# The sample's 64x64 triangular inverses built from 16-blocks instead of 32-blocks

## The chip, the core and the metric

The kernel runs on one core of one Trainium2 chip. The metric is the device time of one execution in microseconds. The engines it uses are TensorE (PE: matrix products, with weight loads as PEld), VectorE (DVE), ScalarE (ACT), GpSimd (POOL) and the queues that issue transfers (SP). Each engine runs its own list of instructions in order and waits on semaphores for the others.

## What is computed

Two layers of a mixed trunk run on 640 tokens: 128 context tokens and 512 sample tokens. In each layer a projection feeds a short convolution, a windowed attention and a gated delta rule ("DeltaNet") in both directions; then come an output projection and a SwiGLU block. The part that the change touches is the delta rule's chunk solve. With chunks of 64 tokens:

```
lmat = einsum('bhnid,bhnjd->bhnij', kb, kc) * dec_strict        # strictly lower triangular
eye  = jnp.eye(CHUNK)
rhs  = concatenate([vc * bc, kb * exp(gc)], axis=-1)
sol  = triangular_solve(lmat + eye, rhs, lower=True, unit_diagonal=True)
```

The kernel forms the inverse of `lmat + eye` itself, for every chunk, head and direction. The sample has 8 chunks, 4 heads and 2 directions, thus 64 inverses of 64x64 in each layer; the context has 2 chunks, thus 16.

## The kernel before

Tokens lie in 5 tiles of 128: tile 0 is the context (group 0, `nt=1`), tiles 1 to 4 the sample (group 1, `nt=4`). A string of letters per layer (`SEQ`) names the stages in the order in which they are written: `Y` and `y` the decays, `A` and `B` the gram matrices of the keys of sample and context, `n` a DeltaNet projection, `l`/`L` the normalisation of keys, `I` and `J` the two halves of the sample's inverses, `i` all of the context's, `E` scalars, `c` tables, `q` queries, `g` and `h` the q-gram of sample and context, `d` steps of the transposed projection for the attention and gates, `s` and `z` steps of the recurrent scan. A list scheduler in the framework then sets the order in which the instructions of all stages stand on each engine, so that a stage's rows lie among those of its neighbours. Around the change the string reads `...DYAInynlndnEcBqdJghqsddds...disf...`.

The weights come in as f32 and are split on chip in a high part (`whi`, a cast on ACT, L172) and a low part (`wlo`, a subtraction on DVE, L173). Every product of 128x128 blocks is thus three matmuls: L199, L201 and L202 for the form with 320 columns, L616, L617 and L618 for the form with 256. These fill TensorE for nearly all of the time. Everything else that TensorE does in this stage is small: transposes against `ident` (L661, L813), grams of 64x64 tiles (L841), and the 32x32 tiles of the inverses.

The sample's inverses before (`invert32_a`, `invert32_b`): the two 32x32 diagonal blocks of each 64x64 matrix lie one per partition, after a copy into `Ld` (L987) and a transpose into `Ls` (L989, L990). A forward substitution then builds `Ts` in 31 steps of two DVE instructions each (L999 multiplies, L1001 subtracts), every step on what the step before wrote. `invert32_b` transposes `Ts` back into `DD` (L1008, L1009) and `TTq` (L1010, L1011), copies `DD` into `adx` (L1018), multiplies by the off-diagonal blocks on TensorE (L1025, 64 matmuls of 32x32 into the buffer `pkq`), brings the product back (`X`), copies the diagonal blocks into place (`MK`, L1036), multiplies again (L1047, 64 matmuls) and writes the last blocks (L1053).

The context's inverses (`invert_a`, `invert_b` with `gi=0`) already go by 16-blocks: a substitution of 15 steps (L887, L889) on both 16-blocks of a 32-block at once, transposes (L898 to L901), then on TensorE a product with `Ld` (L913), DVE's `Xs` (L916), two more products (L927 into `pmx`, L934 into `pkq`), ACT's `adx` (L937), copies of the finished 32-blocks from `pkq` into `MK` (L943, on DVE and ACT by turns), and from there the step from 32 to 64 as above (L952, L955, L967, L973). So each operation of the changed code runs in the kernel before too, for a group of a quarter of the width.

Buffers in PSUM: `pkq` has one, `pmx` two and `pmm` two. The q-gram (`gram`) also uses `pkq`: four matmul groups, L841, each followed by DVE's L846, which must have read `pkq` before the next L841 can write it.

Of the kernel before, what the change touches and what calls it, by code (L numbers as in the profile page):

```python
# [12 lines left out]
AF = mybir.ActivationFunctionType  # L13
ALU = mybir.AluOpType
# [94 lines left out]
def hybrid_trunk_kernel(  # L109
# [8 lines left out]
    V, A, G, PE = nc.vector, nc.scalar, nc.gpsimd, nc.tensor  # L118
    mm = PE.matmul
# [28 lines left out]
    def pkq():  # L148
        return ps.tile([128, 2, 512], F32, tag="kq", name="pkq", bufs=1)
# [429 lines left out]
    def mixer(l, mp, hs, early_half, fill, first, later):  # L579
# [4 lines left out]
        def wk(dt=F32, name="wk", shape=(128, 1024)):  # L584
            return mp.tile(list(shape), dt, tag="wk", name=name, bufs=WK_BUFS)
# [4 lines left out]
        def sm(tag, name, n, bufs):  # L590
            return mp.tile([128, n], F32, tag=tag, name=name, bufs=bufs)
# [36 lines left out]
        kk_, vv, kqT, MK, MQ = [], [], [], [], []  # L628
# [263 lines left out]
        def invert_b(gi, nt, LT):  # L892
            Ld, Ts = LT
            nu = 4 * nt
            TT = MK[gi]
            TTq = square(flat("TTq"))
            DD = sm("s2", "DD", 512, 2).rearrange("p (u j) -> p u j", j=16)
            V.transpose(DD[0:64].rearrange("p u j -> p j u"), Ts[0:64, :, 0:16].rearrange("p x y -> p y x"))  # L898
            V.transpose(DD[64:128].rearrange("p u j -> p j u"), Ts[64:128, 16:32])
            V.transpose(TTq[0:64].rearrange("p u i -> p i u"), Ts[0:64])  # L900
# [71 lines left out]
                    dst = TT[w_:w_ + 32, :, :, d, (1 - d) * 32:(2 - d) * 32].rearrange("p t h i -> p (t h) i")  # L972
                    A.activation(dst, po[w_:w_ + 32, 0:nu * 32].rearrange("p (u i) -> p u i", i=32), AF.Copy, scale=-1.0)  # L973

        def invert32_a(gi, nt):
            eng = V
            nu = 4 * nt
            Ld = wk(name="Ld", shape=(128, 32, 32))
            if gi == 0:
                G.memset(Ld, 0.0)  # L980
            for d in range(2):
                for I in range(2):
                    for c2 in range(2):
                        src = MK[gi][c2 * 64 + I * 32:c2 * 64 + I * 32 + 32, :, :, d, I * 32:(I + 1) * 32]
                        dst = Ld[d * 64 + I * 32:d * 64 + I * 32 + 32, :, c2 * nu:(c2 + 1) * nu]
                        cpe = A.copy if (d + I + c2) % 2 else V.tensor_copy
                        cpe(dst.rearrange("p i u -> p u i"), src.rearrange("p t h i -> p (t h) i"))  # L987
            Ls = wk(name="Ls", shape=(128, 32, 32))
            V.transpose(Ls[0:64].rearrange("p x y -> p (x y)"), Ld[0:64].rearrange("p i u -> p (i u)"))  # L989
            V.transpose(Ls[64:128].rearrange("p x y -> p y x"), Ld[64:128])  # L990
            Ts = wk(name="Ts", shape=(128, 32, 32))
            tsf = Ts.rearrange("p x y -> p (x y)")
            G.memset(tsf, 0.0)
            G.memset(tsf[:, 0:1024:33], 1.0)
            for y in range(31):
                n = 31 - y
                tmp = sm("e1", "tmp", 256, 2)
                tv = tmp[:, 0:n * (y + 1)].rearrange("p (x c) -> p x c", c=y + 1)
                eng.tensor_tensor(out=tv, in0=Ls[:, y + 1:32, y:y + 1].to_broadcast([128, n, y + 1]),  # L999
                                  in1=Ts[:, y:y + 1, 0:y + 1].to_broadcast([128, n, y + 1]), op=ALU.mult)  # L1000
                eng.tensor_tensor(out=Ts[:, y + 1:32, 0:y + 1], in0=Ts[:, y + 1:32, 0:y + 1], in1=tv, op=ALU.subtract)  # L1001
            return Ts

        def invert32_b(gi, nt, Ts):
            nu = 4 * nt
            TTq = wk(name="TTq", shape=(128, 32, 32))
            DD = wk(name="DD", shape=(128, 32, 32))
            V.transpose(DD[0:64].rearrange("p u j -> p j u"), Ts[0:64].rearrange("p x y -> p y x"))  # L1008
            V.transpose(DD[64:128].rearrange("p u j -> p j u"), Ts[64:128])  # L1009
            V.transpose(TTq[0:64].rearrange("p u i -> p i u"), Ts[0:64])  # L1010
            V.transpose(TTq[64:128].rearrange("p u i -> p i u"), Ts[64:128].rearrange("p x y -> p y x"))  # L1011

            adx = sm("s2", "adx", 512, 2)[:, 0:nu * 32].rearrange("p (u j) -> p u j", j=32)
            for d in range(2):
                for c2 in range(2):
                    r = c2 * 64 + d * 32
                    q_ = d * 64 + d * 32
                    (A.copy if c2 else V.tensor_copy)(adx[r:r + 32], DD[q_:q_ + 32, c2 * nu:(c2 + 1) * nu])  # L1018
            px = pkq()[:, 0]
            for u in range(nu):  # L1020
                t, hq = divmod(u, 4)
                for c2, d in ((0, 1), (0, 0), (1, 1), (1, 0)):
                    r = c2 * 64 + d * 32
                    w_ = c2 * 64 + (1 - d) * 32
                    mm(px[w_:w_ + 32, u * 32:(u + 1) * 32], lhsT=MK[gi][r:r + 32, t, hq, d, (1 - d) * 32:(2 - d) * 32],  # L1025
                       rhs=adx[r:r + 32, u], start=True, stop=True)
            X = sm("s2", "X", 512, 2)
            A.copy(X[:, 0:nu * 32], px[:, 0:nu * 32])
            X = X[:, 0:nu * 32].rearrange("p (u j) -> p u j", j=32)
            TT = MK[gi]  # L1030
            for d in range(2):
                for I in range(2):
                    for c2 in range(2):
                        dst = TT[c2 * 64 + I * 32:c2 * 64 + I * 32 + 32, :, :, d, I * 32:(I + 1) * 32].rearrange("p t h i -> p (t h) i")
                        src = TTq[d * 64 + I * 32:d * 64 + I * 32 + 32, c2 * nu:(c2 + 1) * nu]
                        (A.copy if (d + I + c2) % 2 else V.tensor_copy)(dst, src)  # L1036
            for d in range(2):
                for c2 in range(2):
                    z0 = c2 * 64 + (1 - d) * 32
                    G.memset(TT[z0:z0 + 32, :, :, d, d * 32:(d + 1) * 32], 0.0)  # L1040
            po = pkq()[:, 0]
            for u in range(nu):
                t, hq = divmod(u, 4)
                for c2, d in ((0, 0), (0, 1), (1, 0), (1, 1)):
                    r = c2 * 64 + (1 - d) * 32
                    w_ = c2 * 64 + d * 32
                    mm(po[w_:w_ + 32, u * 32:(u + 1) * 32], lhsT=X[r:r + 32, u],  # L1047
                       rhs=TT[r:r + 32, t, hq, d, (1 - d) * 32:(2 - d) * 32], start=True, stop=True)
            for d in range(2):
                for c2 in range(2):  # L1050
                    w_ = c2 * 64 + d * 32
                    dst = TT[w_:w_ + 32, :, :, d, (1 - d) * 32:(2 - d) * 32].rearrange("p t h i -> p (t h) i")
                    A.activation(dst, po[w_:w_ + 32, 0:nu * 32].rearrange("p (u i) -> p u i", i=32), AF.Copy, scale=-1.0)  # L1053


        KTs = mp.tile([128, 2, 2, 640], F32R, name="KTs", bufs=1)
        KTp = mp.tile([128, 2, 2, 128], F32R, name="KTp", bufs=1)
# [142 lines left out]
        early, oos, held = [], [], []  # L1200
# [282 lines left out]
        for op in SEQ[l]:  # L1483
            if op in 'AB':
                gram(1 if op == 'A' else 0, 1)
            elif op in 'Ll':
                l2(1 if op == 'L' else 0, 1)
            elif op in 'Yy':
                decays(1 if op == 'Y' else 0)
            elif op in '23':  # L1490
                dn_post(int(op), ps_[int(op) - 2])
            elif op == 't':
                z_tile(next(tg))
            elif op == 'D':
                decay_scalars()
            elif op == 'c':
                tables()
            elif op == 'E':
                scan_scalars()
            elif op == 'I':  # L1500
                held.append(invert32_a(1, 4))
            elif op == 'J':
                invert32_b(1, 4, held.pop())
            elif op == 'i':
                invert_b(0, 1, invert_a(0, 1))
            elif op == 'n':
                dn_proj(next(ng))
            elif op in 'gh':
                gi = 1 if op == 'g' else 0
                l2(gi, 0)  # L1510
                gram(gi, 0)
            elif op == 'q':
                queries(next(qg))
            elif op == 'k':
                keys()
            elif op == 'm':
                make_mix()
            elif op == 'f':
                fill(FN)
            elif op == 'w':  # L1520
                part_out(next(wg))
            elif op in 'op':
                dn_output(1 if op == 'o' else 0)
            else:
                drain({'s': s1g, 'z': s0g, 'a': ag, 'd': dg}[op], 1)
# [59 lines left out]
    for l in range(depth):  # L1585
# [6 lines left out]
        with tc.tile_pool(name=f"f{l + 1}", bufs=1, reuse_waits="tile") as fp:  # L1592
# [182 lines left out]
            held = pkq()  # L1775
# [102 lines left out]
```

## Time and profile before

| what | value |
|---|---|
| device time, three runs | 1776.96, 1778.72, 1785.07 us; median 1778.72 |
| profiled execution | 1782.25 us, span 1780.5 us |
| mean granted TensorE clock | 0.974 |
| TensorE busy | 94% of the span |
| weight loads | 84% |
| VectorE busy | 70% |
| ScalarE, GpSimd busy | 44%, 9% |

The shares are means over stages. The stage with the sample's inverses lies from about 98 to 205 us in layer 0 and from about 970 to 1075 us in layer 1. PEclk in a view of windows is the clock that TensorE was granted there, as a share of its full 2.4 GHz; 0.50 is the lower level of 1.2 GHz.

### The profile page before, as it was taken

Reading aid. Unit: us, or ns where it says so; the run is one execution under the profiler, and the core shown is the slowest. Engines: PE = TensorE matmul, PEld = TensorE weight load, DVE = VectorE, ACT = ScalarE, POOL = GpSimd, SP = SyncE. Lnnn points to the kernel's source line nnn. Section 1 sums busy time; section 2 is a strip of 40 time slices with the busy share of each in tenths; the row PEclk is TensorE's granted clock in tenths of the full one; section 3 lists DMA queues with packets and bytes.
Section 4 is the critical chain, followed back from the end, with each engine's and each line's share of the span. In section 5 each row is a group of like instructions: output and inputs, shape, how many; then the busy total and the mean of one; then the engine's idle time right before and its main releaser. Section 6 shows DMA issues by size and latency. Waiting matters only on the chain. (4 is left out here: it accounts for less than half of the span.)

```text
span 1780.5 us, 34163 instructions
## 1 busy us (share of the span) xinstructions
PE 1676.7 (94%) x13677; PEld 1497.3 (84%) x13677; DVE 1242.5 (70%) x2764; ACT 782.7 (44%) x1620; POOL 156.3 (9%) x270
## 2 busy tenths in 40 slices
PE   5998999999999999999999989999998999999998
PEld 3887875478899999999988879655888999999998
DVE  3699767665966767666677994886578766667654
ACT  3555244544643433434355442555365343434332
POOL 1111012102300000000032001120041000000000
PEclk8999999999999999999999989999999999999999
DMA  8512224555534223222232222445722222222212
GB/s 280 187 37 78 72 87 129 185 178 164 155 119 131 81 74 96 72 83 73 71 99 75 63 58 67 151 143 164 233 63 84 83 73 82 83 84 84 73 59 60
DMA packets 207693, 188.42 MB, mean 106 GB/s; under 512 B 12782, under 2 KB 182702, under 8 KB 207534
## 3 DMA queue, kind: packets, MB, share of 16 engines
q1 hardware_dynamic: 190656, 170.71, 31.2%
q10 hardware_dynamic: 16878, 15.53, 2.8%
q8 instruction: 108, 1.77, 0.4%
q14 instruction: 51, 0.42, 0.1%
HBM read 168.64 MB, written 17.56 MB: 105 GB/s over the span
## 5 line engine op out<-in xcount | busy, mean ns | idle before, releaser
L172 ACT CAST whi<-raw 128x1024 fp32r<-128x1024 f32 (+1 forms) x102 | 100.0, 981 | 166.5 <-PE pmx L201 73.5
L173 DVE TENSOR_TENSOR wlo<-raw,whi 128x1024 fp32r<-128x1024 f32 (+1 forms) x102 | 115.9, 1138 | 26.5 <-ACT whi L172 26.0
L202 PE MATMUL pmm<-hh,wlo 128*128 128x320 f32 x336 | 109.4, 327 | 6.6 <-DVE wlo L173 6.5
L199 PE MATMUL pmm<-hh,whi 128*128 128x320 f32 x336 | 109.9, 328 | 4.2 <-ACT dnp L645 2.9
L199 PE MATMUL pmm<-acth,whi 128*128 128x320 f32 x320 | 100.6, 314 | 7.3 <-DVE xt L571 7.3
L571 DVE SCALAR_TENSOR_TENSOR xt<-pmx,mod,xt 128x128 f32<-128x128 f32 (+2 forms) x168 | 68.9, 434 | 51.9 <-PE pmx L202 49.5
L201 PE MATMUL pmm<-hl,whi 128*128 128x320 f32 x320 | 104.0, 325 | 0.0
L199 PE MATMUL pmx<-acth,whi 128*128 128x320 f32 x320 | 99.8, 312 | 1.8 <-DVE xt L571 1.7
L202 PE MATMUL pmm<-acth,wlo 128*128 128x320 f32 x320 | 99.8, 312 | 0.0
L201 PE MATMUL pmx<-actl,whi 128*128 128x320 f32 x320 | 99.7, 312 | 0.0
L202 PE MATMUL pmx<-acth,wlo 128*128 128x320 f32 x320 | 99.6, 311 | 0.0
L201 PE MATMUL pmm<-actl,whi 128*128 128x320 f32 x320 | 99.5, 311 | 0.0
L571 DVE SCALAR_TENSOR_TENSOR xt<-pmm,mod,xt 128x128 f32<-128x128 f32 (+2 forms) x168 | 68.6, 433 | 36.4 <-PE pmm L202 24.4
L172 ACT CAST whi<-rawd 128x1024 fp32r<-128x1024 f32 x40 | 42.0, 1049 | 107.7 <-PE pmx L201 101.6
L372 POOL TENSOR_TENSOR acc<-acc,sq 128x320 f32<-128x320 f32 x24 | 25.8, 1077 | 611.8 <-ACT sq L371 524.5
L202 PEld LDWEIGHTS pmm<-hh,wlo 128*128 128x128 f32 x336 | 66.4, 198 | 8.2 <-DVE wlo L173 7.4
L199 PEld LDWEIGHTS pmm<-hh,whi 128*128 128x128 f32 x336 | 66.5, 198 | 6.2 <-ACT dnp L645 3.8
L617 PE MATMUL pmm<-wlo,hh 128*128 128x256 f32 x240 | 70.2, 292 | 0.5 <-DVE wlo L173 0.4
L616 PE MATMUL pmm<-whi,hh 128*128 128x256 f32 x240 | 70.2, 294 | 0.0
L618 PE MATMUL pmm<-whi,hl 128*128 128x256 f32 x240 | 70.2, 293 | 0.0
L288 PE MATMUL pdn<-adaw,c 128*32 128x256 f32 x640 | 63.2, 396 | 6.2 <-DMA adaw<-in_ada_w_dram 6.0
L199 PEld LDWEIGHTS pmm<-acth,whi 128*128 128x128 f32 x320 | 60.7, 190 | 9.9 <-issue 7.0
(561 smaller groups left out, 5610.9 us busy)
## 6 DMA issues: line engine op xcount, KB each, us to landing
adaw<-in_ada_w_dram SPq DMA_DIRECT2D x80, 512.0 KB, 4.0
raw<-in_w_down_dram SPq DMA_DIRECT2D x44, 512.0 KB, 3.5
raw<-in_w_in_dram SPq DMA_DIRECT2D x36, 512.0 KB, 4.5
rawo<-in_w_gate_dram SPq DMA_DIRECT2D x40, 256.0 KB, 3.4
rawd<-in_w_gate_dram SPq DMA_DIRECT2D x40, 256.0 KB, 3.4
rawo<-in_w_up_dram SPq DMA_DIRECT2D x40, 256.0 KB, 3.4
rawd<-in_w_up_dram SPq DMA_DIRECT2D x40, 256.0 KB, 3.4
araw<-in_ada_w_dram SPq DMA_DIRECT2D x16, 512.0 KB, 6.4
```

What stands on the lines that cost most here:

```text
L172: (hi_eng or A.copy)(hi, src)
L173: (lo_eng or V).tensor_tensor(out=lo, in0=src, in1=hi.bitcast(F32), op=ALU.subtract)
L199: mm(o, lhsT=wh[:, k], rhs=ah, start=k == 0, stop=False)
L201: mm(o, lhsT=wh[:, k], rhs=al, start=False, stop=False)
L202: mm(o, lhsT=wl[:, k], rhs=ah, start=False, stop=not lead and k == n - 1)
L288: mm(pr[32 * q:32 * q + 32, 0:256], lhsT=c32[:, k], rhs=raw[:, q * 256:(q + 1) * 256], start=k == 0, stop=k == 7)
L372: (G if k < 5 else V).tensor_tensor(out=self.acc[h], in0=self.acc[h], in1=sq, op=ALU.add)
L571: V.scalar_tensor_tensor(out=x[:, sl], in0=pt[:, a0:a1], scalar=gate[:, g:g + 1], in1=x[:, sl], op0=ALU.mult, op1=ALU.add)
L616: mm(pt, lhsT=ah[:, ts], rhs=wh[:, k % 4], start=k == 0, stop=False)
L617: mm(pt, lhsT=ah[:, ts], rhs=wl[:, k % 4], start=False, stop=False)
L618: mm(pt, lhsT=al[:, ts], rhs=wh[:, k % 4], start=False, stop=k == 7)
```

## The change

The letters `I` and `J` now call `invert_a(1, 4)` and `invert_b(1, 4, ...)`, the code that the context uses. The functions `invert32_a` and `invert32_b` are gone, so that every line behind L955 has a number that is smaller by 80 (L1067 becomes L987, L1047's work is now at L967, which keeps its number). The solve of the sample has 15 steps instead of 31, and three groups of matmuls are new for it (L913, L927, L934).

```
             elif op == 'I':
-                held.append(invert32_a(1, 4))
+                held.append(invert_a(1, 4))
             elif op == 'J':
-                invert32_b(1, 4, held.pop())
+                invert_b(1, 4, held.pop())
```

```
-            for y in range(31):
-                n = 31 - y
-                tmp = sm("e1", "tmp", 256, 2)
-                tv = tmp[:, 0:n * (y + 1)].rearrange("p (x c) -> p x c", c=y + 1)
-                eng.tensor_tensor(out=tv, in0=Ls[:, y + 1:32, y:y + 1].to_broadcast([128, n, y + 1]),
-                                  in1=Ts[:, y:y + 1, 0:y + 1].to_broadcast([128, n, y + 1]), op=ALU.mult)
-                eng.tensor_tensor(out=Ts[:, y + 1:32, 0:y + 1], in0=Ts[:, y + 1:32, 0:y + 1], in1=tv, op=ALU.subtract)
...
-            V.transpose(DD[0:64].rearrange("p u j -> p j u"), Ts[0:64].rearrange("p x y -> p y x"))
-            V.transpose(DD[64:128].rearrange("p u j -> p j u"), Ts[64:128])
-            V.transpose(TTq[0:64].rearrange("p u i -> p i u"), Ts[0:64])
-            V.transpose(TTq[64:128].rearrange("p u i -> p i u"), Ts[64:128].rearrange("p x y -> p y x"))
...
-                    (A.copy if c2 else V.tensor_copy)(adx[r:r + 32], DD[q_:q_ + 32, c2 * nu:(c2 + 1) * nu])
-            px = pkq()[:, 0]
...
-                        (A.copy if (d + I + c2) % 2 else V.tensor_copy)(dst, src)
```

In its place `invert_a` and `invert_b`, which stand in full above, run with `nt=4` and `nu=16`: L913 with 128 matmuls into `pkq`, two L916 on DVE, L927 with 64 matmuls into `pmx` and L934 with 128 into `pkq` (4 and 8 by turns), one L937 on ACT, four L943, L952 with 64 matmuls (as L1025, but into `pmx`), one L955, L967 with 64 (as L1047), four L973.

On TensorE in layer 0, at the end of the 320-column matmuls, the kernel before has the first part of the sample's product with `adx` (the name of the 32-blocks' inverses):

```order
L618 MATMUL pmm<-whi,hl 128x256
L1025 MATMUL pkq<-adx,MK 32x32 x2
L199 MATMUL pmm<-hh,whi 128x320
L201 MATMUL pmm<-hl,whi 128x320
L1025 MATMUL pkq<-adx,MK 32x32 x33
L202 MATMUL pmm<-hh,wlo 128x320
```

and, 45 rows of 320-column matmuls later, the last product:

```order
L616 MATMUL pmm<-whi,hh 128x256
L617 MATMUL pmm<-wlo,hh 128x256
L1047 MATMUL pkq<-MK,X 32x32 x64
L813 MATMUL pmx<-ident,qd 128x128 x8
L618 MATMUL pmm<-whi,hl 128x256
```

In the kernel after, the 16-block product (`DD` and `Ld`) stands at the first place:

```order
L618 MATMUL pmm<-whi,hl 128x256
L199 MATMUL pmm<-hh,whi 128x320
L201 MATMUL pmm<-hl,whi 128x320
L913 MATMUL pkq<-DD,Ld 32x16 x27
L202 MATMUL pmm<-hh,wlo 128x320
```

and the steps from 32 to 64 come behind, after L927 and L934, among the 256-column matmuls and the transposes of the queries `qd`:

```order
L618 MATMUL pmm<-whi,hl 128x256
L952 MATMUL pmx<-adx,MK 32x32 x64
L813 MATMUL pmx<-ident,qd 128x128 x4
L616 MATMUL pmm<-whi,hh 128x256
L617 MATMUL pmm<-wlo,hh 128x256
L813 MATMUL pmx<-ident,qd 128x128 x5
L618 MATMUL pmm<-whi,hl 128x256
L616 MATMUL pmm<-whi,hh 128x256
L617 MATMUL pmm<-wlo,hh 128x256
L618 MATMUL pmm<-whi,hl 128x256
L616 MATMUL pmm<-whi,hh 128x256
L967 MATMUL pkq<-MK,X 32x32 x64
```

All of the 32-block product has thus moved behind the 320-column matmuls, and the last one stands 67 rows later than before.

On VectorE in layer 0 the kernel before ends the solve and goes straight to the transposes and `adx` (L1067 is a row sum for the attention, L173 the low part of a weight):

```order
L1001 TENSOR_TENSOR Ts<-Ts,tmp 128x31
L1008 STREAM_TRANSPOSE DD<-Ts 64x32x32
L1009 STREAM_TRANSPOSE DD<-Ts 64x32x32
L1067 TENSOR_REDUCE qss<-asq 128x4
L1010 STREAM_TRANSPOSE TTq<-Ts 64x32x32
L1011 STREAM_TRANSPOSE TTq<-Ts 64x32x32
L1018 COPY adx<-DD 32x512 x2
L1067 TENSOR_REDUCE qss<-asq 128x4
L1036 COPY MK<-TTq 32x16x32 x3
L173 TENSOR_TENSOR wlo<-raw,whi 128x1024
```

In the kernel after, the same end of the solve stands earlier, among the convolution of the DeltaNet projection (`dny`, L603, L604, L657), which stood within the solve before:

```order
L889 TENSOR_TENSOR Ts<-Ts,tmp 128x2x15
L603 SCALAR_TENSOR_TENSOR dny<-dnp,vec_126,dny 128x642
L898 STREAM_TRANSPOSE DD<-Ts 64x16x32
L604 SCALAR_TENSOR_TENSOR dny<-dnp,vec_126,dny 128x642
L899 STREAM_TRANSPOSE DD<-Ts 64x16x32
L900 STREAM_TRANSPOSE TTq<-Ts 64x32x32
L657 SCALAR_TENSOR_TENSOR dny<-dnp,dny 128x642
L901 STREAM_TRANSPOSE TTq<-Ts 64x32x32
L173 TENSOR_TENSOR wlo<-raw,whi 128x1024
L846 TENSOR_TENSOR MK<-pkq,MQ 128x256
```

`adx` is no longer made on DVE, and one L657 now stands behind three transposes. Later on DVE, the context's solve (L887 and L889) and the q-gram's L846 are interleaved in the kernel before with the first L846 after eight steps:

```order
L887 TENSOR_TENSOR tmp<-Ls,Ts 128x126
L227 TENSOR_TENSOR rsz<-rsx,rsy 128x4
L889 TENSOR_TENSOR Ts<-Ts,tmp 128x2x9x7
L229 TENSOR_TENSOR rsw<-rsz,rsy 128x4
L887 TENSOR_TENSOR tmp<-Ls,Ts 128x128
L846 TENSOR_TENSOR MQ<-pkq,MQ 128x256 x2
```

In the kernel after the context's solve starts only behind the sample's L943:

```order
L916 SCALAR_TENSOR_TENSOR Xs<-pkq,cst 64x32x16
L987 TENSOR_REDUCE qss<-asq 128x4
L943 COPY MK<-pkq 32x32x32
L880 STREAM_TRANSPOSE Ls<-Ld 64x1024
L943 COPY MK<-pkq 32x32x32
L881 STREAM_TRANSPOSE Ls<-Ld 64x32x32
L887 TENSOR_TENSOR tmp<-Ls,Ts 128x30
L889 TENSOR_TENSOR Ts<-Ts,tmp 128x2x15
```

and its first L846 of the q-gram comes after nine of the fifteen steps:

```order
L889 TENSOR_TENSOR Ts<-Ts,tmp 128x2x8x8
L887 TENSOR_TENSOR tmp<-Ls,Ts 128x126
L889 TENSOR_TENSOR Ts<-Ts,tmp 128x2x7x9
L846 TENSOR_TENSOR MQ<-pkq,MQ 128x256 x2
L987 TENSOR_REDUCE qss<-asq 128x4
L887 TENSOR_TENSOR tmp<-Ls,Ts 128x120
```

The place of the first L846 in the context's solve is about the same, but the solve as a whole has moved behind the sample's last steps.

## Rows read from the trace of the kernel before

**Rows 1.** The page, part 1: busy us, share of the span, instructions of each engine.

```profile
PE 1676.7 (94%) x13677; PEld 1497.3 (84%) x13677; DVE 1242.5 (70%) x2764; ACT 782.7 (44%) x1620; POOL 156.3 (9%) x270
```

**Rows 2.** Windows (length, busy us per engine (instructions), PEclk, DMA share, GB/s), layer 0.

```profile
150.00:160.00 10.00, 5.22 (x104) 4.71 (x102) 9.77 (x11) 8.28 (x15) 0.96 (x1) 0.95 0.12 40
```

**Rows 3.** Waits of PE, layer 0 (us in total, times, longest).

```profile
PE pmm L202 <- DVE wlo L173: 4.0, 2, 2.0
PE pkq L1025 <- DVE adx L1018: 3.4, 1, 3.4
PE pmx L813 <- DVE qd L808: 2.6, 1, 2.6
```

**Rows 4.** Waits of PE, layer 1.

```profile
PE pkq L1025 <- DVE adx L1018: 2.9, 1, 2.9
PE pmm L202 <- DVE wlo L173: 2.5, 1, 2.5
PE pmx L813 <- DVE qd L808: 2.1, 1, 2.1
...
PE pmm L199 <- ACT whi L172: 1.2, 1, 1.2
```

**Rows 5.** Windows of the stretches at the lower clock, both layers.

```profile
160.60:165.60 5.00, 4.99 (x19) 4.99 (x20) 4.81 (x13) 0.09 (x1) 0.96 (x1) 0.50 0.75 207
175.00:180.00 5.00, 4.41 (x30) 4.28 (x30) 4.55 (x19) 1.62 (x3) 0.00 (x0) 0.66 0.41 108
1028.50:1032.60 4.10, 4.10 (x15) 4.10 (x16) 3.97 (x7) 0.00 (x0) 0.00 (x0) 0.50 0.71 189
1045.00:1053.00 8.00, 7.61 (x62) 6.58 (x62) 5.59 (x28) 1.26 (x3) 0.00 (x0) 0.59 0.01 2
1067.00:1074.00 7.00, 6.38 (x34) 5.54 (x34) 4.15 (x12) 0.30 (x1) 0.00 (x0) 0.52 0.53 157
```

**Rows 6.** Lines on DVE (line, op, tiles, shapes, count | busy, mean ns | idle before).

```profile
L1001 DVE TENSOR_TENSOR Ts<-Ts,tmp 128x31 f32<-128x31 f32 (+15 forms) x62 | 21.1, 341 | 1.0
...
L889 DVE TENSOR_TENSOR Ts<-Ts,tmp 128x30 f32<-128x30 f32 (+7 forms) x30 | 7.6, 253 | 0.4
...
L900 DVE STREAM_TRANSPOSE TTq<-Ts 64x1024 f32<-64x1024 f32 x2 | 4.2, 2083 | 0.0
...
L898 DVE STREAM_TRANSPOSE DD<-Ts 64x512 f32<-64x512 f32 x2 | 2.4, 1182 | 0.1
```

**Rows 7.** Timeline of PE, context's products (start us, us, instruction, records).

```profile
256.32 0.75 PE L913 MATMUL pkq<-DD,Ld 32*32 32x16 f32 x40
257.00 1.05 PE L288 MATMUL pdn<-adaw,c 128*32 128x256 f32 x10
257.98 0.26 PE L927 MATMUL pmx<-Xs,TTq 32*32 32x32 f32 x6
...
258.94 0.64 PE L288 MATMUL pdn<-adaw,c 128*32 128x256 f32 x8
```

**Rows 8.** Timeline of PE, 256-column matmuls and the sample's last product, layer 0.

```profile
171.31 0.28 PE L616 MATMUL pmm<-whi,hh 128*128 128x256 f32 x1
171.43 0.28 PE L617 MATMUL pmm<-wlo,hh 128*128 128x256 f32 x1
171.73 1.29 PE L1047 MATMUL pkq<-MK,X 32*32 32x32 f32 x128
```

**Rows 9.** Lines on DVE: copies of two widths out of PSUM.

```profile
L1421 DVE COPY pp<-pmx 128x512 f32<-128x512 f32 x28 | 19.3, 688 | 11.3 <-PE pmx L1418 11.0
...
L943 DVE COPY MK<-pkq 32x256 f32<-32x256 f32 x4 | 1.7, 416 | 0.9 <-ACT MK L943 0.9
```

**Rows 10.** Lines on ACT: the same two widths.

```profile
L1421 ACT COPY pp<-pmx 128x512 f32<-128x512 f32 x32 | 18.8, 588 | 22.6 <-PE pmx L1418 22.6
...
L943 ACT COPY MK<-pkq 32x256 f32<-32x256 f32 x4 | 1.5, 364 | 2.1 <-DVE MK L943 2.1
```

**Rows 11.** Window behind the context's inverses, layer 0.

```profile
265.00:270.00 5.00, 5.00 (x56) 2.88 (x54) 3.58 (x12) 2.46 (x9) 0.99 (x2) 0.68 0.30 70
```

More of the change, by code (lines that the diff above doesn't have):

```diff
@@ L973, in invert_b @@
                     A.activation(dst, po[w_:w_ + 32, 0:nu * 32].rearrange("p (u i) -> p u i", i=32), AF.Copy, scale=-1.0)
[L975 to L994, printed above, removed]
-            for y in range(31):
-                n = 31 - y
-                tmp = sm("e1", "tmp", 256, 2)
-                tv = tmp[:, 0:n * (y + 1)].rearrange("p (x c) -> p x c", c=y + 1)
-                eng.tensor_tensor(out=tv, in0=Ls[:, y + 1:32, y:y + 1].to_broadcast([128, n, y + 1]),
-                                  in1=Ts[:, y:y + 1, 0:y + 1].to_broadcast([128, n, y + 1]), op=ALU.mult)
-                eng.tensor_tensor(out=Ts[:, y + 1:32, 0:y + 1], in0=Ts[:, y + 1:32, 0:y + 1], in1=tv, op=ALU.subtract)
-            return Ts
@@ L1004, in invert32_b @@
[L1004 to L1007, printed above, removed]
-            V.transpose(DD[0:64].rearrange("p u j -> p j u"), Ts[0:64].rearrange("p x y -> p y x"))
-            V.transpose(DD[64:128].rearrange("p u j -> p j u"), Ts[64:128])
-            V.transpose(TTq[0:64].rearrange("p u i -> p i u"), Ts[0:64])
-            V.transpose(TTq[64:128].rearrange("p u i -> p i u"), Ts[64:128].rearrange("p x y -> p y x"))
[L1013 to L1017, printed above, removed]
-                    (A.copy if c2 else V.tensor_copy)(adx[r:r + 32], DD[q_:q_ + 32, c2 * nu:(c2 + 1) * nu])
-            px = pkq()[:, 0]
[L1020 to L1035, printed above, removed]
-                        (A.copy if (d + I + c2) % 2 else V.tensor_copy)(dst, src)
[L1037 to L1053, printed above, removed]
```

## Prediction

> **What bounds the kernel now.** I read four views in this order. The page's first part says that TensorE is busy for 94% of the span [rows 1], so an edit pays only where TensorE waits or runs at the lower clock, and costs whatever it adds to TensorE. The windows of the stage say something else about VectorE, whose share over the whole kernel is 70%: between 150 and 160 us it is busy for 9.8 of 10 us and TensorE for only 5.2 [rows 2]. There VectorE sets the end. The waits of TensorE name the places. In layer 0 the product with `adx` waits 3.4 us, two matmuls with `wlo` wait 2.0 us each, and the transposes of `qd` 2.6 us [rows 3]; in layer 1 the same list has 2.9, 2.5 and 2.1, and a wait of 1.2 for `whi` [rows 4]. Last come the windows behind these waits: PEclk is 0.50 (1.2 GHz) from 160.6 to 165.6 us, 0.66 from 175 to 180, and in layer 1 0.50, 0.59 and 0.52 in three stretches [rows 5]. Before each of them TensorE stood idle.
>
> What these stretches lose I take as (1 - PEclk) times the busy time: 2.5 and 1.5 us in layer 0; 2.05, 3.1 and 3.05 us in layer 1. That is a little too much, since part of a matmul's pace is not the clock's.
>
> **What the change removes on VectorE.** L999 and L1001 take 21.1 us each over two layers [rows 6], thus 21.1 us per layer for both. Their 31 steps become 15 with the two instructions of which one (L889) is at 253 ns in the context's solve [rows 6], and L887 alike; the shapes are the same for the wider group, since the matrices lie one per partition and column. So 30 x 0.26 = 7.8 us stand in place of 21.1, and 13.3 us per layer go. The transposes into `DD` are halved in width: 1.18 us [rows 6] in place of twice that, a pair of them, thus another 2 us. In return come two L916, two L943 of 1.2 us each, all later in the order.
>
> What TensorE gets from it, up to the end of the 320-column matmuls: the `adx` wait goes (3.4 and 2.9), since `DD` is ready long before TensorE gets there; the `wlo` or `whi` wait behind it goes (2.0 and 1.2), since VectorE and ScalarE reach those splits earlier; with no idle stretch the lower clock behind them goes too (2.5 and 2.05). That is 7.9 us in layer 0 and 6.15 in layer 1. Late next is the convolution: one L657 now stands behind L898, L899 and L900, and the transposes L661 of TensorE wait for it. The three transposes are 1.18, about as much, and 2.08 us [rows 6], together 4.3 us, which is the upper bound; the lower is zero, if VectorE is by then that far ahead. Walking both engines through the changed order with the durations of before I get 1.6 us of waiting in layer 0, and take 1.0 for each layer, because the walk starts from a VectorE that is already full.
>
> **What it adds to TensorE.** New per layer: 128 matmuls of L913, 64 of L927 and 128 of L934. The trace records each of them twice. In the context's stage 40 records of L913 take the 0.68 us from 256.32 to 257.00, 17 ns each; L927 and L934, 96 records, take the 0.96 us from 257.98 to 258.94, 10 ns each [rows 7]. The sample's own 32-block product has the same 10 ns (128 records in 1.29 us [rows 8]). So L913 costs 256 x 17 ns = 4.35 us and the other two 384 x 10 ns = 3.85 us. L952 and L967 cost what L1025 and L1047 did. Sum: 8.2 us per layer, on an engine which has no other work missing there; nothing hides it but the waits that go.
>
> The 17 ns may hold the edges of a short group. The Trainium skill, TensorEngine Tiling (Array Packing), section Key Properties, speaks against this change in that way: a change of the tiling mode drains TensorE, and the changed order has more groups of 32x32 tiles between 128x128 matmuls. No row shows a drain by itself. If the 7 ns over the others' 10 were all edges, L913 in its two long groups would cost some 2.6 us plus those edges, about 3 us, and the sum below would be some 2.5 us lower over both layers; by the rows as they stand it is the 4.35 above.
>
> **What comes behind.** The product with `adx` and everything after it now lies behind the 320-column matmuls, where the queries' part of the stage was. The `qd` wait goes, since L808 stands early on VectorE now (2.6 and 2.1 us). Three waits come.
> First, the chain from L927 over ScalarE's `adx` (0.59 us at the sample's width of 512, as L1421 [rows 10]) and `X` to L967 and the buffer `pkq`: behind each step only a few matmuls stand on TensorE. I take 1.3 us in all, from 0.4, 0.5 and 0.4.
> Second, the four L943 go from engine to engine: in the rows of the context DVE's waits for ACT's and ACT's for DVE's [rows 9, 10]. At four times the width, by the rise from 256 to 512 columns (0.416 to 0.688 on DVE, 0.364 to 0.588 on ACT [rows 9, 10]), one takes 1.23 and 1.04 us, and the four 4.5 us. On TensorE, L952 (1.3 us, as L1047 [rows 8]), nine transposes and thirteen 256-column matmuls at 0.12 us [rows 8] lie between L934 and L967, with the transposes at the pace of the others some 4 us, so this is nearly covered; what is not is in the 1.3. If nothing covered it, it would be 4.5 us per layer.
> Third, the q-gram. The context's solve stands behind L943 on VectorE and the first L846 behind nine of its steps: two transposes of 3.2 us together (L880 and L881, as L898 and L900 [rows 6]), 9 x 0.52 = 4.7 us, then L846, while TensorE needs L846 to free `pkq` for the second L841. The walk gives 1.7 us; bounds 0 and 4.7.
> The `wlo` wait at the end (2.0 and 2.5) stays: the same context transposes stand ahead of it. The lower clock behind the old `qd` wait stays in layer 0, since new waits stand there, and I let half of it go in layer 1 (1.5 of 3.1).
>
> **The sum.** Layer 0: 8.2 - 7.9 - 2.6 + 1.0 + 1.3 + 1.7 = +1.7 us. Layer 1: 8.2 - 6.15 - 2.1 - 1.5 + 1.0 + 1.3 + 1.7 = +2.45 us. Together about +4.2 us on an execution of 1782.25 us (span 1780.5), so 1786.4; that execution lay 3.5 us above the median of the runs, and on the median of 1778.72 it is 1783.
>
> **The rivals.**
> Faster: VectorE's freed 13.3 us per layer reach every wait. TensorE finds its operands ready, all waits of rows 3 and 4 in this stage go, and the clock stays up. Layer 0: 8.2 - 7.9 - 2.6 - 1.5 - 2.0 = -5.8; layer 1: 8.2 - 6.15 - 2.1 - 3.1 - 2.5 - 3.05 = -8.7; together -14.5, thus 1764. For it speaks that VectorE is full in this stage; against it that the freed time lies ahead of the 320-column matmuls' end, and the new chain behind it.
> Slower: the clock. Each of the three new waits leaves TensorE short of work in a stretch of small products, and the lower clock follows, as behind the context's inverses, where 265 to 270 us has 0.68 [rows 11], a loss of 1.6 us, and behind the `qd` wait. At 1.5 to 3.1 us for each, two more such stretches per layer at 2.3 us add 9.2 us to the sum: +13.4, thus 1792. It decides from the point where PEclk is below 0.8 in a second stretch between L934 and the last L841. For it: each of the old waits of 2 us and more was followed by one [rows 5]. Against it: the new waits are shorter than 2 us by the walk.
> No effect of the kind meant: VectorE's relief is real, but TensorE would have reached `adx` just as late because ScalarE's casts `whi` gate it. Then layer 0 loses 2.0 + 2.5 us more than I count, layer 1 1.2 + 2.05, and the time is 1783 + 7.75 = 1791. ScalarE is busy for 8.3 of 10 us there [rows 2], which speaks for it; that its casts wait for VectorE's release of buffers speaks against it.
>
> **How the numbers follow.** My sum 0.5, the faster rival 0.2, the clock 0.2, the casts 0.1. About 0.5% (8.9 us) is what a measurement of this kernel tells from no change, so faster begins below 1769.8 and slower above 1787.6. My own sum has bounds of some -6 to +8 us from the waits taken by the walk (1.0, 1.3 and 1.7 per layer) and from L913, which puts a tenth of it on the slower side; of the rivals on that side about nine tenths lie beyond 1787.6. That gives faster 0.2, same 0.48, slower 0.32. The range from 1765 to 1797 leaves a tenth out at either end.
>
> **What would show it.** L999 and L1001 gone, and L887 and L889 at 60 instructions each with about 255 ns. TensorE's wait on `adx` L1018 gone, and none longer than 0.5 us at the first L913; PEclk at 1.00 behind it. L913 at 17 ns per record and L927 with L934 at 10. A wait of 1 to 2 us at the second L841 with L846 as its releaser, one of up to 1.6 us at L661 with L657. I am wrong if L913 in its long groups runs at another pace, if a second stretch at the lower clock follows L934, or if the waits at L661 and L841 are absent.

## The result and the profile after

The changed kernel takes 1797.3 us (median of five runs, 1794.52 to 1810.98) against 1778.72: slower by a ratio of 1.0125 with a 95% interval of 1.0094 to 1.0156 (1.0104 by the two medians). The forecast was 1783, which is no clear change, in a range of 1765 to 1797; the time lies just above the top of the range. The profiled execution is the longest of the five (span 1809.2 us), so stages are compared here, not spans.

The page of the kernel after, parts 1 and 3 (part 3: queue, packets, MB, share of the engines):

```profile
PE 1696.6 (94%) x14957; PEld 1516.1 (84%) x14957; DVE 1220.5 (67%) x2696; ACT 781.3 (43%) x1614; POOL 163.9 (9%) x274
...
q8 instruction: 118, 1.93, 0.5%
```

and the same queue in the kernel before:

```profile
q8 instruction: 108, 1.77, 0.4%
```

TensorE has 1280 matmul records and 1280 weight loads more than in [rows 1], as the working said: 320 new matmuls of the program per layer, each of which stands as two records and two loads, thus four instructions. VectorE lost 22 us of work. The last line is the one that counts: the queue on which TensorE's own instructions come has ten packets more, at 1.77 MB / 108 = 16 KB each. 2560 instructions in 10 packets make 256 in each, which is 64 of the program's small matmuls.

Waits of TensorE in the kernel after, first layer 0 (95 to 215 us) and then layer 1 (980 to 1105 us), against [rows 3, 4]:

```profile
PE pkq L934 <- issue: 3.8, 2, 2.0
PE pmx L927 <- issue: 2.7, 1, 2.7
PE pmm L199 <- ACT dnp L645: 2.1, 1, 2.1
PE pmx L661 <- DVE dny L657: 2.0, 1, 2.0
PE pmm L202 <- DVE wlo L173: 2.0, 2, 1.2
...
PE pmx L661 <- DVE dny L657: 2.9, 2, 1.9
PE pmx L927 <- issue: 2.8, 1, 2.8
PE pkq L934 <- issue: 2.4, 1, 2.4
```

The waits on `adx` and `qd` are gone. In their place stand waits that no engine ends: "issue" says that the profile shows nothing that TensorE waited for. They lie inside L927 and L934, groups of matmuls whose operands have been there since the first of them ran. The windows of TensorE, cut at these stalls (length, busy us and matmul records, PEclk, DMA share, GB/s), show the pattern:

```profile
172.70:175.75 3.05, 2.93 (x126) 1.00 0.06 16
175.75:177.65 1.90, 0.00 (x0) 1.00 0.18 57
177.65:179.00 1.35, 1.28 (x128) 1.00 0.00 0
179.00:181.65 2.65, 0.00 (x0) 0.58 0.02 6
181.65:183.35 1.70, 1.60 (x128) 0.50 0.04 10
183.35:185.10 1.75, 0.00 (x0) 0.50 0.00 0
185.10:188.35 3.25, 3.15 (x128) 0.50 0.02 5
```

The bursts have 128 matmul records (the last with some large matmuls among them), which with their 128 weight loads are 256 instructions: one packet of the instruction queue. A burst at full clock lasts 1.28 us, and the bursts start 3.5 to 4.0 us apart (177.68, 181.69, 185.14). That TensorE stands still until the next packet has come is borne out by the view of the queues from 175 to 186.2 us, in 40 slices of 0.28 us:

```profile
GB/s 0 59 194 242 7 7 18 0 0 0 0 0 0 0 0 59 0 0 0 0 0 0 0 0 0 0 0 59 0 0 0 0 0 0 0 0 0 0 0 0
...
q8 instruction: 3, 0.05, 1.7%
```

59 GB/s in a slice is one packet of 16 KB. The three such slices begin at 175.3, 179.2 and 182.6 us, each 2.4 to 2.6 us ahead of a restart. Other transfers can hardly hold the packets up: from 177.65 us on the queues are busy for 0.00 to 0.04 of the time. In the second stall the granted clock falls to 1.2 GHz, and the windows of ten microseconds that answer to [rows 5] (PE, PEld, DVE, ACT, POOL, then PEclk) show how long it stays there:

```profile
170.00:180.00 10.00, 6.48 (x294) 5.88 (x287) 3.52 (x5) 1.62 (x3) 1.29 (x3) 0.97 0.24 69
180.00:190.00 10.00, 6.16 (x279) 5.53 (x279) 4.36 (x4) 2.18 (x3) 0.00 (x0) 0.50 0.02 5
190.00:200.00 10.00, 9.81 (x211) 9.12 (x211) 8.31 (x27) 5.66 (x11) 0.00 (x0) 0.85 0.05 15
```

VectorE, which was full in this stage, is at 3.5 and 4.4 of 10 us here, waiting for L934. The Trainium skill, Runtime: NRT & Kernel Launch, section Instruction fetch mechanics, says that each engine's instructions are refilled in blocks of 16 KiB, 256 instructions, and that crossing a block's edge is mostly hidden. The trace agrees with the block and its size. It does not agree that the edge is hidden, where 256 instructions run in 1.28 us and the next come only 1.9 to 2.7 us later.

The lines on VectorE that answer to [rows 6]:

```profile
L889 DVE TENSOR_TENSOR Ts<-Ts,tmp 128x30 f32<-128x30 f32 (+7 forms) x60 | 15.6, 260 | 1.2
...
L898 DVE STREAM_TRANSPOSE DD<-Ts 64x512 f32<-64x512 f32 x4 | 4.8, 1189 | 0.1
```

The solve costs what was forecast: 60 instructions of 260 ns in L889 (and 60 of 253 in L887), and L999 and L1001 (21.1 us each) are gone.

### The profile page after: what moved, and what is told of

It is laid out like the page before. It is cut to its first block, busy times and chain, and to the rows that moved or that the text cites. A ratio compares the mean times of both kernels' runs of the same rounds, so it can differ in the third digit from the quotient of the medians.

```text
span 1809.2 us, 36644 instructions
## 1 busy us (share of the span) xinstructions
PE 1696.6 (94%) x14957; PEld 1516.1 (84%) x14957; DVE 1220.5 (67%) x2696; ACT 781.3 (43%) x1614; POOL 163.9 (9%) x274
## 5 line engine op out<-in xcount | busy, mean ns | idle before, releaser
L173 DVE TENSOR_TENSOR wlo<-raw,whi 128x1024 fp32r<-128x1024 f32 (+1 forms) x102 | 115.9, 1138 | 36.3 <-ACT whi L172 35.8
L202 PE MATMUL pmm<-hh,wlo 128*128 128x320 f32 x336 | 108.0, 323 | 4.0 <-DVE wlo L173 4.0
L202 PE MATMUL pmm<-acth,wlo 128*128 128x320 f32 x320 | 99.5, 311 | 0.0
L202 PE MATMUL pmx<-acth,wlo 128*128 128x320 f32 x320 | 99.1, 310 | 0.0
L172 ACT CAST whi<-rawd 128x1024 fp32r<-128x1024 f32 x40 | 42.0, 1049 | 105.7 <-PE pmx L201 99.9
L202 PEld LDWEIGHTS pmm<-hh,wlo 128*128 128x128 f32 x336 | 65.0, 194 | 5.6 <-DVE wlo L173 4.7
L617 PE MATMUL pmm<-wlo,hh 128*128 128x256 f32 x240 | 69.6, 291 | 0.0
```

What stands on the lines that cost most here:

```text
L172: (hi_eng or A.copy)(hi, src)
L173: (lo_eng or V).tensor_tensor(out=lo, in0=src, in1=hi.bitcast(F32), op=ALU.subtract)
L202: mm(o, lhsT=wl[:, k], rhs=ah, start=False, stop=not lead and k == n - 1)
L617: mm(pt, lhsT=ah[:, ts], rhs=wl[:, k % 4], start=False, stop=False)
```

## The experiments

To read all kernels alike I take two marks in TensorE's list that stand in each: the last matmul of the decays (L828), ahead of the sample's solve is used, and the first transpose of the keys (L1112, L1032 after the change), behind the stage. The stage is the time from one to the other, read from the timelines of each run's profile. The times are medians of the runs, the ratios are against runs of the kernel before on the same chips. The stage is from one profiled execution each, and the time outside the two stages lies up to 11 us off before's, so the differences of the stages and of the medians agree only roughly.

| kernel | stage, layer 0 | stage, layer 1 | median us | ratio to before (95%) |
|---|---|---|---|---|
| before | 103.2 | 106.1 | 1778.7 | |
| after | 115.2 | 112.1 | 1797.3 | 1.0125 (1.0094 to 1.0156) |
| few | 107.6 | 105.7 | 1791.4 | 1.0057 (1.0036 to 1.0078) |
| double | 128.7 | 121.5 | 1829.0 | 1.0264 (1.0219 to 1.0310) |
| split | 112.2 | 110.9 | 1798.8 | 1.0103 (1.0072 to 1.0133) |
| coarse | 107.7 | 103.6 | 1783.9 | 1.0028 (1.0006 to 1.0050) |
| early | 112.7 | 109.1 | 1796.4 | 1.0080 (1.0051 to 1.0110) |
| solve15 | 102.4 | 104.3 | 1777.8 | 0.9984 (0.9964 to 1.0004) |
| solve15_pool | 104.0 | 104.0 | 1781.2 | 1.0006 (0.9990 to 1.0022) |
| solve1 | 98.9 | 101.2 | 1776.9 | 0.9971 (0.9950 to 0.9991) |

**Fewer instructions, same columns (few).**

```
-            for u in range(nu):
+            gw = 4 if gi else 1
+            for u in range(0, nu, gw):
...
-                        mm(pa[..., u * 32:(u + 1) * 32], lhsT=TTq[rows, c2 * nu + u], rhs=Xs[rows, c2 * nu + u], ...)
+                        mm(pa[..., u * 32:(u + gw) * 32], lhsT=TTq[rows, c2 * nu + u], rhs=Xs[rows, c2 * nu + u:c2 * nu + u + gw], ...)
```

and L934 likewise.

> The kernel after, with L927 and L934 of the sample in groups of four columns blocks: 48 matmuls of 128 columns in place of 192 of 32 (the values of these products are other ones; columns streamed, buffers and waits are the same). Theory F, instruction supply: TensorE's instructions come in blocks of 16 KB, 256 of them, and a block takes some 3.5 us to follow another; the stalls of 2.0, 2.7 and 1.9 us inside L927 and L934 each come after exactly 256 records. 768 instructions per layer become 192, so these stalls go: 6 to 8 us less per layer, 1781 to 1785 us. Rival P, price of the products (pace per column, drains at the edges of the groups): 3.85 us become some 2.6 per layer, about 1794 us, stalls stay.

The stage is 7.6 and 6.4 us shorter than after's, where theory F had 6 to 8. In the trace of few, TensorE's waits from 165 to 195 us are:

```profile
PE pkq L968 <- issue: 1.6, 1, 1.6
PE pmx L928 <- DVE Xs L916: 0.5, 1, 0.5
PE pmx L953 <- issue: 0.3, 1, 0.3
```

No stall on instructions is left inside L928 and L935, which are L927 and L934 here. A stall of 1.6 us stands at L968, the next group of 64 small matmuls. The queue has 113 packets, five fewer (4.5 by the count of instructions). The whole kernel is at 1791, outside the 1781 to 1785 that I named for F: the two stages are 14 us shorter than after's, the median is 6 us lower, by the ratios it is 12. The time alone does not decide against the price of the products (rival P), which had 1794; the trace does, since P had the stalls in place.

**The same products twice (double).**

```
-            for u in range(nu):
+            for u in list(range(nu)) * (2 if gi else 1):
```

> The kernel after, with L927 and L934 of the sample written twice over (same values). Theory F: 768 more instructions per layer in one stretch, three blocks of 256, each 3.5 us: +10.5 us per layer, about 1818 us; and three more idle stretches of 2 us and more between them, each after 256 records. Rival P: 384 more records per layer at 10 ns, +3.85 us per layer, about 1805 us.

13.6 and 9.4 us more per stage than after, where F had +10.5 per layer and P +3.85. The whole kernel is at 1829, above both forecasts (1818 and 1805). What layer 0 has over F's 10.5 fits the clock: PEclk is 0.50 from 180 to 200 us here, where after has 0.85 from 190 to 200. The stalls in the timeline of double, layer 0 (start, us, instruction, records, idle time before):

```profile
177.48 0.23 PE L934 MATMUL pkq<-TTq,Xs 32*32 32x32 f32 x3 [2.00 <-issue]
...
181.48 0.27 PE L927 MATMUL pmx<-Xs,TTq 32*32 32x32 f32 x3 [2.73 <-issue]
...
185.21 0.30 PE L934 MATMUL pkq<-TTq,Xs 32*32 32x32 f32 x8 [2.12 <-issue]
...
189.21 0.27 PE L934 MATMUL pkq<-TTq,Xs 32*32 32x32 f32 x3 [2.39 <-issue]
...
193.21 0.27 PE L927 MATMUL pmx<-Xs,TTq 32*32 32x32 f32 x3 [2.42 <-issue]
...
196.94 0.35 PE L934 MATMUL pkq<-TTq,Xs 32*32 32x32 f32 x14 [2.12 <-issue]
```

Three more, at a steady 3.7 to 4.0 us from one restart to the next, and sometimes L927 is the one to wait, sometimes L934: what counts is the number of instructions, not the line. The page counts 124 packets, six more, for 1536 more instructions: 256 each.

**The products in small pieces (split).** `invert_b` became a generator that the large matmuls step on:

```
+    def tick():
...
+        side["owed"] += side["rate"]
+        while side["owed"] > 0:
+            try:
+                side["owed"] -= next(side["gen"])
...
             mm(o, lhsT=wl[:, k], rhs=ah, start=False, stop=not lead and k == n - 1)
+            tick()
...
-  'DYAInynlndnEcBqdJghq...'
+  'DYAInynlndnEcBZghq...'      (Z: q and one d, which is a step of the short convolution, with J inside)
```

> The kernel after with the same instructions for the inverses, but written in pieces among the 256-column matmuls of the first queries and the 320-column ones that follow, 32 instructions' worth behind every three large matmuls. Theory F: no stretch of TensorE needs a block of 256 in much under 3.5 us, so the stalls go and the relief of VectorE stays: 1765 to 1778 us. Rival P: the same products cost the same, with some 40 more changes between small and large tiles: 1797 us or more, by 0.2 us a change up to 1810.

The stalls went, as F said (none in layer 0, one of 0.5 us in layer 1), and the time did not: 1798.8, where F had 1765 to 1778 and P 1797 or more. F alone falls short. What the pieces cost stands in the timeline of split, at one of twelve such pieces per layer:

```profile
157.11 0.28 PE L633 MATMUL pmm<-whi,hl 128*128 128x256 f32 x1
157.32 0.23 PE L944 MATMUL pmx<-Xs,TTq 32*32 32x32 f32 x4
...
157.58 0.39 PE L631 MATMUL pmm<-whi,hh 128*128 128x256 f32 x1
157.80 0.28 PE L632 MATMUL pmm<-wlo,hh 128*128 128x256 f32 x1
157.92 0.28 PE L633 MATMUL pmm<-whi,hl 128*128 128x256 f32 x1
158.13 0.23 PE L944 MATMUL pmx<-Xs,TTq 32*32 32x32 f32 x4
```

From this piece to the next it is 0.81 us. Three large matmuls at 0.12 us take 0.36 and 24 small records at 10 ns 0.24; 0.21 us are left for going to the small tiles and back: a large matmul is followed by the small one after 0.21 instead of 0.12 us, and the first large one behind them by the next after 0.22. The Trainium skill, TensorEngine Tiling (Array Packing), section Key Properties, says that a change of tiling mode drains TensorE; the trace agrees in that a visit costs 0.21 us more than its records; it does not show the drain itself.

**Pieces of a packet's size (coarse).**

```
         side["owed"] += side["rate"]
+        if side["owed"] < PIECE:
+            return
```

with `PIECE = 256`, so that a piece is written only when 256 instructions are owed.

> As split, but in pieces of about 64 matmuls (256 instructions) with some 24 large matmuls between them: 11 groups of small tiles per layer in place of some 45. Theory F with E (blocks of 256 instructions, and a price of 0.21 to 0.26 us for each visit of TensorE to the small tiles, as split's trace has it): no stall on instructions and 34 visits less per layer, 7 to 9 us, so 1780 to 1786 us. F without E: as split, 1797. Rival P (the products have one price wherever they stand): 1797.

1783.9 us, in the range of F with E. The order has ten groups of small tiles per layer, split has 38 (I had said 11 and some 45); 56 visits fewer in two layers for 14.9 us between the medians are 0.27 us each; by the ratios it is 0.24, by the two stages 0.21. Both prices together, and neither alone, fit after's time, split's and this one, with the same instructions for the inverses in all three. TensorE's waits from 140 to 180 us, where all the products lie, are down to:

```profile
PE pkq L953 <- issue: 1.5, 1, 1.5
PE pmm L218 <- DVE wlo L174: 0.2, 1, 0.2
```

**The same stretches elsewhere (early).**

```
-  'DYAInynlndnEcBqdJghq...'
+  'DYAInynlndnEcBJqdghq...'
```

> The kernel after with J written ahead of the queries and the short convolution: the products stand some 110 large matmuls earlier, in stretches as long as before (36, 192 and 64 matmuls). Theory F: the place doesn't matter, the stalls of 2 to 2.7 us after each 256 records stay, 5 to 7 us per layer, about 1797 us (1790 to 1802). Rival W (what is lost behind the 320-column matmuls is the chain of waits through Xs, adx, MK and the q-gram's buffer): with 110 large matmuls to hide the chain it is about 1785 us.

1796.4 us: the place does not help, as F said. Waits of TensorE in layer 0:

```profile
PE pmx L927 <- issue: 2.5, 1, 2.5
...
PE pkq L913 <- issue: 1.7, 1, 1.7
...
PE pkq L934 <- issue: 0.8, 1, 0.8
PE pmx L952 <- issue: 0.6, 1, 0.6
PE pkq L967 <- issue: 0.4, 1, 0.4
```

6.0 us in five stalls (5.0 in layer 1). The chain through `Xs`, `adx` and `MK` (rival W) does not appear.

**VectorE's relief alone (solve15, solve1, solve15_pool).**

```
-            for y in range(31):
+            for y in range(16, 31):         (solve15)
+            for y in range(30, 31):         (solve1)
```

> The kernel before, with the last 15 of the 31 steps of the sample's solve alone (the first 16 are left out, so the inverses are not the reference's). Nothing is added to TensorE: it measures what VectorE's relief alone is worth. By the terms of the prediction (waits on adx, wlo and qd and the clock behind them go) some 18 us less than before, about 1760. If the relief only reaches the end of the 320-column matmuls as far as it did in the kernel after (3.5 and 4.1 us), about 1771.

> The kernel before with one of the 31 steps of the sample's solve (30 are left out, other inverses): VectorE is rid of some 20 us per layer and TensorE gets nothing more to do. By the prediction's terms all waits on adx, wlo and qd go, 18 us or more less, 1760 or below. Theory R0 (another wait takes the place of each, as in solve15 and solve15_pool): at most 3 to 5 us less, 1775 to 1780.

Here the prediction's largest gain failed. VectorE's work falls by 19.3 us over both layers in solve15 (22 in the change) and by 36.2 in solve1. With half of the steps gone the kernel is the same within its interval (forecast: about 1760), and with 30 of 31 gone it gains 0.3%. The stage becomes 0.7 and 1.7 us shorter in solve15, 4.2 and 4.9 in solve1. The waits of TensorE in solve15, layer 0 (95 to 215 us), against [rows 3]:

```profile
PE pmm L202 <- DVE wlo L173: 2.5, 1, 2.5
PE pmm L616 <- ACT whi L172: 2.3, 1, 2.3
PE pkq L841 <- DVE MQ L846: 2.2, 2, 1.9
...
PE pmm L617 <- issue: 1.2, 1, 1.2
PE pmm L617 <- DVE wlo L173: 1.0, 1, 1.0
```

The names are others, and the sum of all is hardly smaller: 11.9 us, for 12.3 before. The first theory for it was that ScalarE's casts stand behind its copies from VectorE's transposes:

```
-                        (A.copy if (d + I + c2) % 2 else V.tensor_copy)(dst, src)
+                        (G.tensor_copy if (d + I + c2) % 2 else V.tensor_copy)(dst, src)
```

and the same for the copies of L1018.

> As solve15 (15 of the 31 steps, other inverses), with the four copies each of L1018 and L1036 that stood on ScalarE moved to GpSimd. Theory R (VectorE's relief is lost in order: the casts to whi stand on ScalarE behind copies that wait for VectorE's transposes): the waits on whi (2.3 and 3.4 us) and on the wlo behind it go, some 6 us, about 1772. Rival R0 (another wait takes their place): 1776 to 1780.

It fell. The wait on `whi` went, and one of 4.5 us on the `wlo` behind it took its place:

```profile
PE pmm L617 <- DVE wlo L173: 4.5, 1, 4.5
PE pmm L202 <- DVE wlo L173: 2.5, 1, 2.5
```

In solve1 next to nothing of the solve is left to stand in the way, and a `wlo` still comes 2.5 us late at the first of the 320-column matmuls with `wlo` (L202 at 159.99 us). On VectorE the context's solve, which was later work, has moved ahead of it, in the time that was freed:

```profile
155.20 2.08 DVE L881 STREAM_TRANSPOSE Ls<-Ld 64x1024 f32<-64x1024 f32 x1
157.32 0.42 DVE L1067 TENSOR_REDUCE qss<-asq 128x4 f32<-128x256 f32 x1
...
158.71 1.22 DVE L173 TENSOR_TENSOR wlo<-raw,whi 128x1024 fp32r<-128x1024 f32 x1
```

**Two tries at a better order (before_pool, coarse_hp, before_hp).** The copies on GpSimd in the kernel before:

> The kernel before with the same copies on GpSimd. Theory R: here the copies wait for the end of a solve twice as long, adx comes no earlier, 1777 to 1782. If ScalarE, busy for 8.3 of 10 us between 150 and 160 us, held the stage, some 4 us less.

1782.2 us, ratio 0.9996 (0.9974 to 1.0018): no change. And the convolution's and the grams' instructions put ahead:

```
-            y = conv3(p, vl[:, 70 + m:71 + m], ..., "dny")
+            with tc.high_priority():
+                y = conv3(p, vl[:, 70 + m:71 + m], ..., "dny")
```

with its tanh, L657 and L846, in coarse and in before:

> As coarse, with the instructions of the DeltaNet convolution (L603, L604, L657 and its tanh) and of the grams (L846) put ahead of others where they are ready. Coarse still waits 3.1 and 2.9 us per layer on L657 and 2.7 and 2.7 us on L846 or the context's solve ahead of it. If these waits are owed to the order of VectorE's list alone, 6 to 10 us less than coarse, 1774 to 1778 us, which would be under before. If others take their place, as in solve15, 1784.

> The kernel before with the same order put on those instructions: what of coarse_hp is owed to the order and not to the change. Before waits for neither of them for long in layer 0 and 1.9 us on L657 in layer 1, so 1778 to 1781 us; if the solve is pushed back by it, up to 1784.

1783.7 us, 1.0015 (0.9998 to 1.0032), and 1779.7 us, 0.9999 (0.9979 to 1.0020). Neither differs from the kernel that it was made from by more than the interval. No version that computes the same values beat the kernel before; what would make VectorE's freed time reach TensorE stays open.

## Why the prediction was wrong, step by step

**The price of the products.** Right as far as the pace goes: 101 matmuls of L913 (202 records) take 3.1 us, 15 ns per record for 17, and inside a packet L927 and L934 run at 10 ns. The sum of 8.2 us per layer "on an engine which has no other work missing there" left out that the instructions have to come. Stalls on them are 2.0 + 2.7 + 1.9 + 0.3 = 6.9 us in layer 0 and 2.8 + 2.4 + 0.6 + 0.8 = 6.6 us in layer 1; few, double and coarse show that they are owed to the number of instructions in one stretch. This is the failed step that made the kernel slower: without most of the stalls, in coarse, the ratio to before is 1.0028. The trace of before had one such stall in the context's own small groups, which I read past (TensorE's waits from 257 to 264 us):

```profile
PE pkq L967 <- issue: 1.3, 1, 1.3
```

I took the context's prices per record from groups that are a quarter as long, too short to run through more than one packet. The edge of a visit, of which the working said that no row shows it, stood in [rows 8]: L1047 starts 0.30 us behind L617, where one large matmul follows the other in 0.12.

**VectorE's relief.** Up to the end of the 320-column matmuls I had 6.9 and 5.15 us net. From the first mark to the last L202 of that block it is 50.5 us before (119.08 to 169.62) and 47.0 after (120.05 to 167.06), 3.5 us; in layer 1 48.9 (988.15 to 1037.09) and 44.3 (1006.42 to 1050.70), 4.7 us (the expectation of solve15 has 4.1 there). Layer 0 lost half of the gain, layer 1 little. The wait on `adx` went as forecast. In layer 0 the wait at L661 came, 2.0 us for the 1.0 in the sum; a `wlo` wait of 0.8 stayed; and the lower clock behind it stayed too (PEclk 0.66 from 158 to 163 us, with 4.18 us of work, thus 1.4 us by the prediction's own formula). That is 3.2 of the 3.4 us that are missing.

That VectorE's shorter solve is what gave the rest isn't shown. Up to the same last L202 solve15 takes 50.4 us (115.05 to 165.46) and 52.4 (980.92 to 1033.28), solve1 47.8 in both layers (120.46 to 168.23, 987.48 to 1035.29): with nearly the whole solve gone the gain is 2.8 and 1.1 us, less than after's. So at least a part of after's gain there is not the solve's; the products with `adx` have also moved behind that place. Other waits take the place of each that goes; whether that is because the stage has several chains of nearly one length, or because the scheduler spends the freed time on other work, is not separated.

**What comes behind.** From there to the second mark the prediction had +8.6 us in layer 0 and +7.6 in layer 1; it is +15.6 (52.6 to 68.2) and +10.7 (57.1 to 67.8). In layer 0 the excess over the working is 7.0 us with stalls of 6.9, in layer 1 3.1 us with stalls of 6.6; that the first two agree is in part luck, since other terms changed too. The third wait, the q-gram's on L846 (1.7 in the sum), did not come; in coarse, without most of the stalls, waits of 1.5 and 1.2 us stand there. The `wlo` wait at the end is 1.2 us in both layers for 2.0 and 2.5. In layer 1 these two come to 3.0 of the 3.5 us by which the stalls exceed that excess; the rest I did not trace. In layer 0 they come to 2.5, and against them stands the lower clock, 4.6 us by the prediction's formula (0.50 of 6.16 and 0.15 of 9.81, from 180 to 200 us) for the 1.5 that was left in. The `qd` wait went, as said. The copies L943 go by turns at 1.2 and 1.0 us, as estimated.

**The clock.** PEclk was 0.50 from 180 to 190 us, behind stalls of 2 us and more on instructions, not behind three short waits, so the slower rival had the right sign, almost the right time (1792), and another cause than the one that I gave it; its nearness is luck. Its argument that each old wait of 2 us and more was followed by the lower clock was a misreading: the second `wlo` wait of [rows 3] (2.0 us, at 198.29 us) was not, PEclk is 1.00 from 190 to 210 us. In the kernel after it is still 1.00 in the burst behind the first stall of 2.0 us.

**The casts.** No wait on `whi` stands in either stage of the kernel after, so this rival did not come, though its 1791 was near too.

**The range.** 1797 was its top and the time is 1797.3. The chance of 0.32 for slower was too low: no rival had a price for the supply of instructions, and I counted the relief as known, though no run had shown that a wait that ends on VectorE goes when VectorE has less to do.

## What to carry to other kernels

Small matmuls have a price per instruction that their duration doesn't show: where TensorE ran through 256 instructions (64 small fp32 matmuls of the program, 128 in the trace's records, with their loads) in 1.28 us, the next 256 were late, and the stretch cost 3.5 to 4 us per 256. Write such groups in pieces of about 64 matmuls with some 3 us of large ones between them (here 1783.9 us for 1797.3), and no finer, since each visit to small tiles costs 0.2 to 0.3 us. And before a gain is put down to a wait that goes, halve the work behind it in a throw-away kernel: here that gave a ratio of 0.9984, with 1 inside its interval.

## What the runs showed of the hardware

- Instructions come to TensorE in packets of 16 KB, 256 of them, on a queue of their own. A restart comes 3.5 to 4.0 us after the one before where only small matmuls stand between, with idle stretches of 1.9 to 2.8 us (after and double); the profile calls them "issue". The packet moves some 2.4 us ahead of the restart (after, 175 to 186.2 us).
- A visit of TensorE to 32x32 tiles among 128x128 ones cost 0.21 us in the timeline of split, and 0.21 to 0.27 us by the difference of split and coarse, which are 28 visits per layer apart.
- A stretch of such stalls was followed by a granted clock of 1.2 GHz (after: 0.50 from 180 to 190 us; double: 0.50 from 180 to 200 us).
